# Weight buffers at five different byte offsets, and linear attention begun six parts of a step later

## The chip, the cores and the metric

The kernel runs on one core of a Trainium2 chip. The metric is the device time of one execution in microseconds (us). Before the change it is 2220.42 us, the median of 3 runs (2219.68 to 2222.28).

## What is computed

A two-layer decoder trunk on 256 tokens with 2048 channels, in float32. The reference, cut to its skeleton:

```
for layer in range(2):
    h = rmsnorm(x, norm_mix_g[layer])
    if layer == 0: mix = conv_gla_mixer(h, ...)      # short convolution and gated linear attention
    else:          mix = dilated_attention(h, ...)   # 16 heads, three dilated windows
    x = x + mix
    x = x + square(relu(rmsnorm(x, norm_mlp_g[layer]) @ w1[layer])) @ w2[layer]
return rmsnorm(x, final_norm_g)

def conv_gla_mixer(h, ...):
    a_b, a_c, a_x, q, k, v, r, g_low = split(h @ w_in)
    y_conv = a_b * causal_short_conv(a_c * a_x, conv_w)
    log_a  = log_sigmoid(g_low @ w_gate2 + b_gate) / 16
    o = rmsnorm(gla_chunked(q, k, v, log_a), gla_norm_g) * silu(r)
    return concat([y_conv, o]) @ w_out
```

Nearly all of the work is the products with the large weight matrices: `w_in`, `w_out`, `w_qkv`, `w_o`, and `w1` and `w2` of both MLPs (D_FF is 8192).

## The kernel before

**Weights in steps.** The weights stream through in 769 steps, all but one (step 8, the small gate weight) of one 128x1024 float32 block (512 KB). `load` brings a block into one of four `raw` buffers through the SP queue. `split_high` (ScalarE, L139) writes the block rounded to float32r into a buffer `wh`; `split_low` (VectorE, L152) writes what the rounding left off into a buffer `wl`. There are five buffers of each (WB = 5), used in turn. The loop at L796 splits four steps ahead (LA = 4).

**The products.** A step of the commonest kind ("a", `sub_a`) makes 24 matmuls of 256 columns: for each of 8 pieces of the block the three products `wh` x high, `wh` x low and `wl` x high of an activation tile (`xs`, `ys` or `hs`, whose high and low halves lie side by side). All go through `mm`, so all stand under L155. The weights are the loaded (stationary) operand, the activations the streamed one. Steps of kind "b" (the v projections) have the roles the other way round, with 512 columns streamed.

**Parts.** The loop cuts a step into four parts (j = 0 to 3; six matmuls each in kind "a"). After each part `advance()` counts one and resumes at most one background generator whose time has come. `spawn(gen, after)` enters a generator that starts `after` parts later, and a generator's `yield n` puts it off by n parts. So the place of all small work in the engines' queues (norm factors, gates, linear attention, attention heads) is fixed by counting parts when the program is written, not at run time.

**Linear attention.** `evac_glow` leads, through `after_norm` and `gates`, to the log gates `la`: small matmuls `pz`, then Abs, Exp and Ln on ScalarE (L428 to L430), then two operations on VectorE (L433). `gla_pair(pair)` handles two heads; its first work is four plain float32 matmuls `pg` that read `la` (L446), then `G` (L450), and from there eight rounds of exponentials (`E`), products (`W`) and scores (`psc`), and at the end `po`, `pos` and `porb`. Pair 0 is entered by the trigger at the first step after its v projection (step 17), six parts later; pair 1 in the same way at step 49. Such plain float32 matmuls also occur at the norm factors (`pss`, `prb`) and in the attention heads.

**Addresses.** Tiles of a pool lie one behind the other in the order in which their tags are first asked for. `fill` (88 floats) brings the `const` pool, with `x`, `xs`, `ys` and `hs`, to a multiple of 2 KiB, and `fill2` (16 floats) puts everything in the weight pool 64 bytes past one: all four `raw`, all five `wh` and all five `wl` buffers lie at 64 modulo 2048. The activation halves `xs`, `ys` and `hs` lie at 0 and 1024.

Of the kernel before, what the change touches and what calls it, by code (L numbers as in the profile page):

```python
# [11 lines left out]
F32 = mybir.dt.float32  # L12
F32R = mybir.dt.float32r
# [5 lines left out]
P = 128  # L19
# [30 lines left out]
def trunk_kernel(ctx: ExitStack, tc, xin, vecs, w_in, w_gate, w_gate2, w_out, w_qkv, w_o, w1, w2, w2f,  # L50
# [9 lines left out]
    wts = ctx.enter_context(tc.tile_pool(name="wts", bufs=1))  # L60
# [4 lines left out]
    RAW, WB, LA, WARM = 4, 5, 4, 5  # L65
# [7 lines left out]
    ident, cums = cm[:, 0, :], cm[:, 1, :]  # L73
    ones = small.tile([P, 1], F32, name="ones")
    small.tile([P, 88], F32, name="fill")
    wts.tile([P, 16], F32, name="fill2")
    x = const.tile([P, NK, T], F32, name="x")

# [30 lines left out]
    steps = []  # L109

    def add(g):
        for i in range(g.n):
            steps.append((g, i))

    raws, his, los = {}, {}, {}

    def parts(s):
        return (slice(0, 512), slice(512, 1024)) if s == 0 else (slice(0, 1024),)
# [11 lines left out]
    def split_high(s):  # L130
        if steps[s][0].kind == "h":
            r = raws[s][:, :256].rearrange("p (k c) -> p k c", c=16)
            for q in range(4):
                act.activation(wg3[q][:, :, :16], r[:, 4 * q:4 * q + 4, :], AF.Copy)
            his[s] = None
            return
        his[s] = wts.tile([P, 1024], F32R, tag="wh", bufs=WB, name=f"wh{s}")
        for c in parts(s):
            act.activation(his[s][:, c], raws[s][:, c], AF.Copy)  # L139

    def split_low(s):
        r = raws.pop(s)
        if steps[s][0].kind == "h":
            r = r[:, :256].rearrange("p (k c) -> p k c", c=16)
            for q in range(4):
                dve.tensor_tensor(wg3[q][:, :, 32:48], r[:, 4 * q:4 * q + 4, :],
                                  wg3[q][:, :, :16].bitcast(F32), op=OP.subtract)
            los[s] = None
            return
        los[s] = wts.tile([P, 1024], F32R, tag="wl", bufs=WB, name=f"wl{s}")  # L150
        for c in parts(s):
            dve.tensor_tensor(los[s][:, c], r[:, c], his[s][:, c].bitcast(F32), op=OP.subtract)  # L152

# [93 lines left out]
    def spawn(gen, after=1):  # L247
        bg.append([gen, clock[0] + after])
# [125 lines left out]
    def evac_qk(pair):  # L374
        def f(j, p):
            if j == 0:
                gl["q", pair] = gpool.tile([P, 2, T], F32, tag="gq", bufs=2, name="gq")
                gl["k", pair] = gpool.tile([P, 2, T], F32, tag="gk", bufs=2, name="gk")
            u = grab(p) if pair == 0 else p

            def rest():
                if j < 2:
                    dve.scalar_tensor_tensor(gl["q", pair][:, j, :], u, DK ** -0.5, R["b"],
                                             op0=OP.mult, op1=OP.mult)
                else:
                    dve.tensor_tensor(gl["k", pair][:, j - 2, :], u, R["b"], op=OP.mult)
            if pair == 0:
                spawn(after_norm(rest))
            else:
                rest()  # L390
        return f
# [7 lines left out]
    def evac_v(store, i):  # L399
        def f(tt, p):  # L400
            if tt == 0:
                store[i] = (ap_["p"] if ap_ else gpool).tile([P, 2, 512], F32, tag="v", bufs=2, name="v")
            act.activation(store[i][:, tt, :], p, AF.Copy, scale=R["c"][:, tt:tt + 1])
        return f
# [171 lines left out]
    def evac_r(half):  # L576
        def f(j, p):
            u = grab(p)
            n = 4 * half + j

            def rest():
                if n == 0:
                    gl["r"] = gpool.tile([P, 8, T], F32, name="r")
                pool.tensor_tensor(gl["r"][:, n, :], u, R["b"], op=OP.mult)
            later.append(rest)
        return f
# [139 lines left out]
    triggers = {}  # L726

    for pair in range(2):
        add(Group(w_in, 32 * pair, 8, "a", X, evac_qk(pair)))
        if pair == 0:  # L730
            add(Group(w_gate, 0, 1, "h", X, evac_glow))
        add(Group(w_in, 32 * pair + 8, 8, "b", X, evac_v(gl["v"], pair)))
        triggers[len(steps)] = lambda pair=pair: spawn(gla_pair(pair), 6)
        if pair == 0:
            add(Group(w_in, 16, 8, "a", X, evac_r(0)))
            add(Group(w_in, 24, 8, "a", X, evac_r(1)))
# [30 lines left out]
    for s in range(LA):  # L767
        first_scale(s)
        split_high(s)
        split_low(s)  # L770
        load_x(s + 4)
        load(s + RAW)
# [23 lines left out]
    for s, (g, i) in enumerate(steps):  # L796
# [6 lines left out]
        if s + LA < len(steps):  # L803
            split_high(s + LA)
        f, n = SUB[g.kind]
        wh, wl = his.pop(s), los.pop(s)
        for j in range(n):
            f(g, i, j, wh, wl)
            if j == 1:
                if s + LA < len(steps):  # L810
                    split_low(s + LA)
                if s + LA + RAW < len(steps):
                    load(s + LA + RAW)
            flush()
            if i == g.n - 1:
                if g.kind == "a" and j % 2 == 1:
                    g.evac(j - 1, part_of(g, j - 1))
                    g.evac(j, part_of(g, j))
                    del g.ps[j // 2]
                elif g.kind == "b" and j % 2 == 1:  # L820
                    g.evac(j // 2, g.ps.pop(j // 2))
                elif g.kind == "g" and j == n - 1:
                    g.evac(0, g.ps.pop(0)[:, :T])
                elif g.kind == "h" and j == n - 1:
                    g.evac(0, g.ps.pop(0))
            advance()
# [100 lines left out]
```

## Time and profile before

| | |
|---|---|
| median of 3 runs | 2220.42 us (2219.68 to 2222.28) |
| the profiled execution | 2219.53 us, of it 2217.7 us span |
| TensorE matmuls (PE) busy | 2199.1 us, 99%, 18358 instructions |
| weight loads (PEld) busy | 2167.6 us, 98% |
| VectorE (DVE) busy | 1323.4 us, 60% |
| ScalarE (ACT) busy | 1038.6 us, 47% |
| mean transfer rate | 185 GB/s |

A busy share of PE says only that some matmul was under way, not how fast matmuls followed each other. A window of the trace gives that: the length of the window over the number of matmuls in it. A plain float32 matmul stands in the trace as two, so `pg` with its four is "x8".

### The profile page before, as it was taken

The page shows a single profiled execution, that of the slowest core. Times are in us where ns is not written, and L with a number is a line of the kernel's source. Part 1 is how long each engine was busy: PE and PEld are TensorE (multiplying, and loading weights), DVE is VectorE, ACT ScalarE, POOL GpSimd, SP SyncE. Part 2 cuts the span into 40 slices and gives each one's busy share as a digit, 9 for nine tenths or more (in the row PEclk, how much of TensorE's full clock was granted, in tenths as well). Part 3 has the DMA queues.
Part 4 walks back from the last instruction along what each step waited for, and adds up shares of the span by engine and source line. Part 5 has one row for each costly group of instructions (what it writes and reads, how often), then busy time and mean ns, then how long its engine had stood idle before and what let it go on. Part 6 is the DMA issues. An engine that isn't in the chain of part 4 may idle for free.

```text
span 2217.7 us, 43336 instructions
## 1 busy us (share of the span) xinstructions
PE 2199.1 (99%) x18358; PEld 2167.6 (98%) x18358; DVE 1323.4 (60%) x1813; ACT 1038.6 (47%) x1416; POOL 69.5 (3%) x75
## 2 busy tenths in 40 slices
PE   9999999999999999999999999999999999999997
PEld 8899999999999999999999999999999999999997
DVE  7566666565555555555755565665555555555555
ACT  5555545453444444354544444545434434534443
POOL 4000230000000000000000000000000000000000
PEclk9999999999999999999999999999999999999999
DMA  7455565666566566656565555565655665566653
GB/s 255 144 170 170 163 199 185 197 192 205 191 198 192 190 198 191 198 179 207 184 194 173 170 165 181 168 198 182 190 184 187 190 183 189 173 200 180 192 189 114
DMA packets 114293, 410.97 MB, mean 185 GB/s; under 512 B 12817, under 2 KB 13329, under 8 KB 114098
## 3 DMA queue, kind: packets, MB, share of 16 engines
q1 hardware_dynamic: 113616, 407.55, 57.9%
q8 instruction: 143, 2.34, 0.4%
q10 hardware_dynamic: 482, 0.65, 0.1%
q14 instruction: 52, 0.43, 0.1%
HBM read 406.05 MB, written 2.10 MB: 184 GB/s over the span
## 4 chain that ended last, share of the span: by engine, by line
PE 98%; DVE 1%; issue 0%; DMA 0%; ACT 0%; SPq 0%; DVEq 0%; ACTq 0%
PE acc L155 88%; PE accv L155 6%; PE accg L155 1%; PE psc L507 1%; PE pao L155 0%; DVE xs L258 0%; PE pqk L642 0%; DVE wl L152 0%; DMA raw<-w_in 0%; PE po L155 0%; PE ppt L669 0%; DVE xf L835 0%; PE pqk L641 0%; PE pos L155 0%; PE pg L446 0%
## 5 line engine op out<-in xcount | busy, mean ns | idle before, releaser
L152 DVE TENSOR_TENSOR wl<-raw,wh 128x1024 fp32r<-128x1024 f32 (+1 forms) x769 | 936.0, 1229 | 733.9 <-ACT wh L139 731.7
L139 ACT ACTIVATE wh<-raw 128x1024 fp32r<-128x1024 f32 (+1 forms) x769 | 810.2, 1058 | 880.5 <-PE acc L155 782.7
L155 PE MATMUL acc<-xs,wh 128*128 128x256 f32 x6400 | 1109.9, 279 | 1.4 <-ACT wh L139 1.1
L155 PEld LDWEIGHTS acc<-xs,wh 128*128 128x128 f32 x6400 | 970.9, 189 | 3.7 <-ACT wh L139 1.9
L155 PE MATMUL acc<-xs,wl 128*128 128x256 f32 x3200 | 882.6, 278 | 1.3 <-DVE wl L152 1.3
L155 PE MATMUL acc<-hs,wh 128*128 128x256 f32 x3968 | 687.7, 278 | 0.0
L155 PEld LDWEIGHTS acc<-hs,wh 128*128 128x128 f32 x3968 | 604.6, 189 | 0.0
L155 PEld LDWEIGHTS acc<-xs,wl 128*128 128x128 f32 x3200 | 597.4, 188 | 1.8 <-DVE wl L152 1.5
L155 PE MATMUL acc<-hs,wl 128*128 128x256 f32 x1984 | 552.4, 278 | 0.0
L155 PEld LDWEIGHTS acc<-hs,wl 128*128 128x128 f32 x1984 | 372.4, 188 | 0.0
L155 PE MATMUL acc<-ys,wh 128*128 128x256 f32 x1024 | 177.6, 278 | 0.0
L155 PEld LDWEIGHTS acc<-ys,wh 128*128 128x128 f32 x1024 | 155.3, 189 | 0.1
L155 PE MATMUL acc<-ys,wl 128*128 128x256 f32 x512 | 142.4, 278 | 0.0
L155 PE MATMUL accv<-wh,xs 128*128 128x512 f32 x384 | 121.0, 396 | 0.0
L330 DVE TENSOR_TENSOR hs<-u,hs 128x256 fp32r<-128x256 f32 x128 | 54.5, 425 | 79.0 <-ACT hs L329 79.0
L155 PEld LDWEIGHTS acc<-ys,wl 128*128 128x128 f32 x512 | 96.1, 188 | 0.0
L329 ACT ACTIVATE hs<-u 128x256 fp32r<-128x256 f32 x128 | 53.4, 417 | 70.1 <-DVE u L697 70.1
L155 PEld LDWEIGHTS accv<-wh,xs 128*128 128x128 f32 x384 | 70.7, 188 | 15.0 <-issue 0.8
L155 PE MATMUL accv<-wl,xs 128*128 128x512 f32 x192 | 75.5, 393 | 0.0
L343 DVE TENSOR_TENSOR x<-x,t 128x256 f32<-128x256 f32 x128 | 54.4, 425 | 4.4
L697 DVE TENSOR_TENSOR u<-u 128x256 f32<-128x256 f32 x128 | 53.5, 418 | 0.0
L341 DVE TENSOR_TENSOR t<-acc,rb 128x256 f32<-128x256 f32 x124 | 51.7, 417 | 0.0
(152 smaller groups left out, 782.4 us busy)
## 6 DMA issues: line engine op xcount, KB each, us to landing
raw<-w SPq DMA_DIRECT2D x504, 512.0 KB, 4.2
raw<-w_qkv SPq DMA_DIRECT2D x96, 512.0 KB, 3.6
raw<-w_in SPq DMA_DIRECT2D x95, 512.0 KB, 3.8
raw<-w_out SPq DMA_DIRECT2D x32, 512.0 KB, 4.1
raw<-w_o SPq DMA_DIRECT2D x32, 512.0 KB, 3.8
raw<-w2f SPq DMA_DIRECT2D x8, 512.0 KB, 3.6
x<-xin SPq DMA_DIRECT2D x8, 256.0 KB, 5.2
out_dram<-xf SPq DMA_DIRECT2D x7, 256.0 KB, 2.3
```

The costliest lines, as they stand in the source:

```text
L139: act.activation(his[s][:, c], raws[s][:, c], AF.Copy)
L152: dve.tensor_tensor(los[s][:, c], r[:, c], his[s][:, c].bitcast(F32), op=OP.subtract)
L155: pe.matmul(out_, lhsT=lhsT, rhs=rhs, start=start, stop=stop, skip_group_check=True)
L329: act.activation(t[:, :T], v, AF.Copy)
L330: dve.tensor_tensor(t[:, T:], v, t[:, :T].bitcast(F32), op=OP.subtract)
L341: dve.tensor_tensor(t, p, R["b2"], op=OP.mult)
L343: dve.tensor_tensor(x[:, k, :], x[:, k, :], p, op=OP.add)
L507: pe.matmul(p[:, (2 * h + tt) * P:(2 * h + tt + 1) * P], lhsT=l[:, h, c], rhs=r[:, h, c], start=True, stop=True)
L697: dve.tensor_tensor(u, u, u, op=OP.mult)
```

## The change

Two edits. First, the buffers `wh` and `wl` get five tags each with one buffer a tag (`wh0` to `wh4`, `wl0` to `wl4`; step s takes number s modulo 5), and ahead of the first use of numbers 1 to 4 a tile of 16 floats (64 bytes) is set aside. So `wh0` and `wl0` stay at 64 modulo 2048, and the next ones lie at 128, 192, 256 and 320. All pools allocated behind the weights (`tmp`, and those of linear attention, attention and the final norm) lie 256 bytes higher. Still a `wh` buffer is reused five steps later, except around step 8, which uses no such buffer. `raw`, `xs`, `ys` and `hs` stay where they were.

Second, both pairs of linear attention are spawned 12 parts after their trigger, where they were spawned 6 after it.

```
@@ split_high
-        his[s] = wts.tile([P, 1024], F32R, tag="wh", bufs=WB, name=f"wh{s}")
+        if 0 < s < WB:
+            wts.tile([P, 16], F32, name=f"stagger{s}")
+        his[s] = wts.tile([P, 1024], F32R, tag=f"wh{s % WB}", bufs=1, name=f"wh{s}")
@@ split_low
-        los[s] = wts.tile([P, 1024], F32R, tag="wl", bufs=WB, name=f"wl{s}")
+        los[s] = wts.tile([P, 1024], F32R, tag=f"wl{s % WB}", bufs=1, name=f"wl{s}")
@@ the triggers
-        triggers[len(steps)] = lambda pair=pair: spawn(gla_pair(pair), 6)
+        triggers[len(steps)] = lambda pair=pair: spawn(gla_pair(pair), 12)
```

On TensorE, before, in step 18 (the digits after `wh` and `wl` are the step's), `pg` of pair 0 stands between the step's second and third part:

```order
L155 MATMUL acc0_722<-xs2_137,wh18_654 128x256 x2
L155 MATMUL acc0_722<-xs2_137,wl18_662 128x256
L155 MATMUL acc0_722<-xs3_143,wh18_654 128x256 x2
L155 MATMUL acc0_722<-xs3_143,wl18_662 128x256
L446 MATMUL pg_772<-cm_73,la_695 128x128 x4
L155 MATMUL acc1_723<-xs2_137,wh18_654 128x256 x2
L155 MATMUL acc1_723<-xs2_137,wl18_662 128x256
```

After the change, on TensorE, it stands between steps 19 and 20 (all line numbers from the `wh` lines on are three higher there):

```order
L158 MATMUL acc1_727<-xs4_157,wh19_676 128x256 x2
L158 MATMUL acc1_727<-xs4_157,wl19_684 128x256
L158 MATMUL acc1_727<-xs5_163,wh19_676 128x256 x2
L158 MATMUL acc1_727<-xs5_163,wl19_684 128x256
L449 MATMUL pg_818<-cm_73,la_699 128x128 x4
L158 MATMUL acc0_726<-xs6_177,wh20_694 128x256 x2
L158 MATMUL acc0_726<-xs6_177,wl20_707 128x256
```

So 36 matmuls of 256 columns (12 of the other half of step 18, 24 of step 19) now stand ahead of `pg` that stood behind it, and every later matmul of linear attention has moved by as many. The matmuls of the weights themselves stand in the order of before.

On ScalarE the same place reads, before, from the log gates on:

```order
L430 ACTIVATE la_695<-la_695 128x1024
L139 ACTIVATE wh21_720<-raw21_646 128x1024
L139 ACTIVATE wh22_754<-raw22_664 128x1024
L450 ACTIVATE G_789<-pg_772 128x512
L139 ACTIVATE wh23_791<-raw23_682 128x1024
```

and after:

```order
L433 ACTIVATE la_699<-la_699 128x1024
L142 ACTIVATE wh21_724<-raw21_650 128x1024
L142 ACTIVATE wh22_758<-raw22_668 128x1024
L142 ACTIVATE wh23_788<-raw23_686 128x1024
L142 ACTIVATE wh24_823<-raw24_709 128x1024
L453 ACTIVATE G_841<-pg_818 128x512
```

Two more weight splits stand ahead of `G`. What leads up to `la` has not moved on any engine, and from the end of pair 1 on (step 81) the order on all engines is the old one. On POOL and in the SP queue nothing has moved at all.

## Rows read from the trace of the kernel before

**Rows 1.** The page: busy time by engine; the ended-last chain's shares by engine.

```profile
PE 2199.1 (99%) x18358; PEld 2167.6 (98%) x18358; DVE 1323.4 (60%) x1813; ACT 1038.6 (47%) x1416; POOL 69.5 (3%) x75
...
PE 98%; DVE 1%; issue 0%; DMA 0%; ACT 0%; SPq 0%; DVEq 0%; ACTq 0%
```

**Rows 2.** Windows around `pg`: us, busy (count) of PE, PEld, DVE, ACT, POOL; PEclk, DMA.

```profile
66.00:69.40 3.40, 0.19 (x3) 0.04 (x1) 0.84 (x2) 3.37 (x5) 0.00 (x0) 0.93 0.00 0
69.40:72.40 3.00, 3.00 (x14) 2.97 (x15) 2.71 (x3) 1.61 (x3) 0.00 (x0) 0.51 0.24 22
72.40:80.00 7.60, 7.60 (x69) 7.60 (x69) 2.61 (x6) 4.18 (x5) 0.00 (x0) 1.00 0.62 198
```

**Rows 3.** Timeline, TensorE, around `pg` of pair 0: start, length, what, [idle before].

```profile
65.91 0.28 PE L155 MATMUL acc<-xs,wl 128*128 128x256 f32 x1
69.39 2.15 PE L446 MATMUL pg<-cm,la 128*128 128x128 f32 x8 [3.21 <-DVE la L433]
71.20 0.77 PE L155 MATMUL acc<-xs,wh 128*128 128x256 f32 x2
71.77 0.41 PE L155 MATMUL acc<-xs,wl 128*128 128x256 f32 x1
71.98 0.56 PE L155 MATMUL acc<-xs,wh 128*128 128x256 f32 x2
```

**Rows 4.** Timeline, `pg` of pair 1, which waits for nothing.

```profile
172.47 1.05 PE L446 MATMUL pg<-cm,la 128*128 128x128 f32 x8
173.27 0.48 PE L155 MATMUL acc<-xs,wh 128*128 128x256 f32 x2
```

**Rows 5.** Timeline, ScalarE and VectorE, the same place as rows 3.

```profile
68.43 1.99 ACT L139 ACTIVATE wh<-raw 128x1024 fp32r<-128x1024 f32 x2
...
68.56 1.29 DVE L433 SCALAR_TENSOR_TENSOR la<-pz,la 128x512 f32<-128x512 f32 x2 [9.24 <-ACT la L430]
69.76 2.35 DVE L152 TENSOR_TENSOR wl<-raw,wh 128x1024 fp32r<-128x1024 f32 x2
```

**Rows 6.** Timeline, the first weighted score of pair 0 and the product it reads.

```profile
81.26 0.41 DVE L494 TENSOR_TENSOR W<-E,gq 128x256 f32<-128x256 f32 x1
...
83.61 1.05 PE L507 MATMUL psc<-W 128*128 128x128 f32 x8
```

**Rows 7.** Windows (columns of rows 2): layer 0 MLP, w_o of layer 1, layer 1 MLP.

```profile
418.00:1098.00 680.00, 680.00 (x6002) 680.00 (x6002) 402.50 (x523) 313.48 (x402) 0.00 (x0) 1.00 0.61 195
...
1411.00:1485.00 74.00, 74.00 (x630) 74.00 (x630) 47.60 (x73) 38.80 (x58) 0.00 (x0) 1.00 0.57 185
...
1498.00:2180.00 682.00, 682.00 (x5793) 1.00 0.59 187
```

**Rows 8.** Groups by line, 430 to 1090, then 1500 to 2180: count | busy, mean ns | idle.

```profile
L155 PE MATMUL acc<-hs,wh 128*128 128x256 f32 x2001 | 340.4, 276 | 0.0
L155 PEld LDWEIGHTS acc<-hs,wh 128*128 128x128 f32 x2002 | 301.4, 188 | 0.0
...
L155 PE MATMUL acc<-hs,wh 128*128 128x256 f32 x1910 | 337.6, 281 | 0.0
L155 PEld LDWEIGHTS acc<-hs,wh 128*128 128x128 f32 x1911 | 295.0, 190 | 0.0
```

**Rows 9.** Timeline, TensorE, norm factors of both MLPs: the small matmuls, the stream after.

```profile
410.48 0.39 PE L155 MATMUL acc<-xs,wh 128*128 128x256 f32 x2
...
410.82 0.50 PE L155 MATMUL pss<-ones,ssq 128*128 128x1 f32 x4
...
411.97 0.40 PE L155 MATMUL acc<-xs,wh 128*128 128x256 f32 x2
...
1490.69 0.50 PE L155 MATMUL pss<-ones,ssq 128*128 128x1 f32 x4
...
1491.48 0.39 PE L155 MATMUL acc<-xs,wh 128*128 128x256 f32 x2
...
1496.58 0.60 PE L310 MATMUL prb<-cm,rc 128*128 128x128 f32 x4
...
1497.38 0.40 PE L155 MATMUL acc<-xs,wh 128*128 128x256 f32 x2
```

## The prediction, made before the changed kernel was run

> **What bounds the kernel now.** I read the page first, then windows of the trace, then the timeline at single places. On the page TensorE is busy 99% of the span and makes up 98% of the chain that ended last [rows 1]; ScalarE and VectorE, at 47% and 60%, wait for it. So there are only two ways to a shorter time: take away one of the few places where TensorE stands still or runs at half clock, or make its matmuls follow each other faster. The change reaches for one of each, and the two have to be judged apart.
>
> The one long standstill away from start and end is at `pg` of linear attention's pair 0. The last weight matmul ahead of it starts at 65.91, `pg` at 69.39, and the row puts 3.21 us of idle time down to the log gates on VectorE [rows 3]. [...] Pair 1 has no such wait: its `pg` starts at 172.47 with no idle time ahead of it [rows 4].
>
> For the pace of the matmuls I divide a window by its count. The MLP of layer 0 makes 6002 matmuls in 680 us, one each 113.3 ns. The MLP of layer 1, the same lines with the same shapes, makes 5793 in 682 us, one each 117.7 ns, and the last projection of layer 1 630 in 74 us, 117.5 ns [rows 7]. So there are two paces, 4.4 ns apart, at a granted clock of 1.00 in both. The groups show them too: a matmul's mean goes from 276 to 281 ns, the loads of `wh` from 188 to 190 ns [rows 8]. And the timeline shows where the pace turns: at plain float32 matmuls. Before `pss` of layer 0 two matmuls take 0.39 us, behind it 0.40; at `pss` of layer 1 it turns the other way (0.39 behind it), and at the following `prb` back to 0.40, where it stays for the rest of the kernel [rows 9]. Between such places it never turns, though the five buffers, the eight pieces of a block and the high and low halves go round all the time.
>
> **Linear attention six parts later.** In front of `pg` now come 36 more matmuls of 256 columns. At 113.3 ns these are 4.08 us, so TensorE reaches `pg` at 65.91 + 0.11 + 4.08 = 70.10 us. The log gates do not depend on anything that moved, and VectorE ends them at 68.56 + 1.29 = 69.85 [rows 5]. The wait is gone, with 0.25 us to spare; were the gates 0.5 us later, it would come back as 0.25 us, not as 3.2.
>
> What that is worth: from 65.91 to 72.38, when the clock is back, TensorE now gets 6 weight matmuls and `pg` done. At the full pace the six are 6 x 0.113 = 0.68 us; `pg` takes 173.27 - 172.47 = 0.80 us at pair 1 [rows 4]; about 0.1 us goes with the first matmul behind it. That is 1.58 us in place of 6.47 [rows 3]: **4.9 us less**, 3.3 of it the wait and the rest the half clock.
>
> What is late next? Two weight splits now stand ahead of `G` on ScalarE, and the splits that were held up behind the log gates (steps 21 and 22) are no longer helped by TensorE standing still. `wh` of these two is there at 68.43 + 1.99 = 70.42 and `wl` at 69.76 + 2.35 = 72.11 [rows 5]; TensorE begins step 21 at 70.10 + 0.9 + 2.72 = 73.7 and step 22 2.7 us later. So they stay covered by 1.6 us or more. The weighted score of pair 0 has its product at 81.26 + 0.41 = 81.67 and starts at 83.61 [rows 6], 1.9 us to spare; the wait in parts between `pg` and it is unchanged, and `G` comes some 1.6 us after `pg` where it now comes 0.4 us after, so even then it is not late. ScalarE's table loads and all of POOL's and SP's work keep their order, so I cost them at nothing. Pair 1 is moved by as much and gains nothing. Bounds of this edit: no gain at all if a wait of 3 us turns up elsewhere, 5.0 us if everything fits.
>
> **Buffers at five offsets.** No instruction is added, none moved, the same buffers are waited for. All that can change is how two streams of addresses, the loaded weights and the streamed activations, meet in memory. The trace of before has float32r weight matmuls at one offset only, so no row gives the price. Bounds from the nearest rows: if every long run took the pace of the layer 0 MLP, 5793 x 4.4 ns = 25.5 us and 630 x 4.2 ns = 2.6 us would go, 28 us in the two windows [rows 7], 30 with their edges; the shorter stretches at the slow pace in attention may add 3. If every long run took the slow pace, the layer 0 MLP would lose 6002 x 4.4 = 26.4 us. So the ends are 33 us of gain and some 26 us of loss (46 if all the projections in the slower pace are added).
>
> Which value? The pace does not turn for whole MLPs while pieces at 64, 576, 1088 and 1600 and halves at 0 and 1024 meet in every combination, and a change of pace needs a float32 matmul in between. Those rows speak for a state of the engine rather than for addresses; the order of the float32 matmuls from step 81 on is unchanged, and so the runs behind them should keep the pace they have. I take **0** as the single likeliest value. But bits of the address below 512 bytes have never varied in this trace, and just those are changed now, so this is the weak step.
>
> [...]
>
> **The sum.** On the profiled execution 2219.5 - 4.9 = 2214.6 us; the median lies 0.9 above that execution, so **2215.5 us** for the median of after.
>
> **The rivals.**
> One, the offsets end the slow pace. For it: the slow pace is a lock that lasts 680 us undisturbed, and a new address relation every 24 matmuls would be the first thing in it to disturb it. The weight loads, of all things, are the rows that lengthen (188 to 190 ns) while it lasts [rows 8]. In full it gives 2215.5 - 30 = 2185, down to 2182 with the attention stretches. In part, if only some of the steps change pace, 2190 to 2212.
> Two, on the other side: the offsets take the layer 0 MLP out of its fast pace. For it: the fast run exists only at offset 64, and four fifths of the buffers leave that offset. In full it gives 2215.5 + 26.4 = 2242. It decides against the change once the steps at the slow pace outnumber those of before by 4.9 us / (24 x 4.4 ns) = 46 of the 768; if two of the five offsets prove slow in the runs that are fast now, it comes to about 2226.
> Three, the first edit doesn't bring what it should, because the log gates or `G` are late again: 2219 to 2221.
>
> **How the numbers follow.** Forecast (2213.5 to 2217) 0.35; rival one in full 0.27, in part 0.16; rival two 0.17; rival three 0.05. The range 2181 to 2232 leaves out the upper half of rival two and little else. About 0.2%, or 4.4 us, is what a measurement of this kernel can tell from no change, so the line is at 2216.0, right beside the forecast. Faster: 0.43 of rival one and 0.21 of the forecast's 0.35, 0.64. Same: 0.14 and 0.04, 0.18. Slower: 0.18.
>
> **What would show it.** The first edit: no idle time ahead of `pg`, a granted clock of 1.00 in the window behind it, and the second layer's work 4.9 us earlier. The second: the counts of matmuls in windows of both MLPs. If they stand at 113.3 and 117.7 ns as before, the forecast holds; if both stand at 113.3, rival one; if pace varies from step to step with the number of the buffer, addresses matter and the forecast's weak step was wrong. A pace below 113.3 ns anywhere would show that I had misread the fast pace as the floor.

## The result, and the profile after

The changed kernel takes **2242.19 us**, the median of 3 runs (2242.11 to 2242.67), against 2220.42 before: a ratio of 1.0097 with a 95% interval of 1.0074 to 1.012. It is slower by 1%, and outside the predicted range of 2181 to 2232.

The page of after, busy time by engine and the shares of the chain that ended last, as in [rows 1]:

```profile
PE 2225.3 (99%) x18358; PEld 2192.9 (98%) x18358; DVE 1324.9 (59%) x1813; ACT 1040.6 (46%) x1416; POOL 64.2 (3%) x75
...
PE 98%; DVE 1%; DMA 0%; issue 0%; SPq 0%; ACT 0%; DVEq 0%; ACTq 0%
```

The same 18358 matmuls, PE busy for the same 99%, and 26.2 us more of it (2225.3 for 2199.1). The other engines have nearly their old busy times. So nothing new is waited for; the matmuls themselves follow each other more slowly.

**Around `pg`** the delay (the second edit in "The change"; the prediction calls it the first) did what was forecast. Windows of after (us, busy (count) of PE, PEld, DVE, ACT and POOL, then PEclk and DMA), which answer to [rows 2]:

```profile
66.00:70.00 4.00, 4.00 (x36) 4.00 (x35) 0.51 (x1) 3.96 (x5) 0.00 (x0) 1.00 0.00 0
70.00:72.50 2.50, 2.50 (x24) 2.50 (x24) 2.50 (x4) 2.50 (x4) 0.00 (x0) 1.00 0.00 0
```

and the timeline of after, TensorE and VectorE, which answers to [rows 3, 5] (start, length, what, and in brackets the idle time before it):

```profile
68.19 0.41 PE L158 MATMUL acc<-xs,wh 128*128 128x256 f32 x2
...
68.56 0.39 PE L158 MATMUL acc<-xs,wh 128*128 128x256 f32 x2
...
71.17 0.28 PE L158 MATMUL acc<-xs,wl 128*128 128x256 f32 x1
71.29 1.05 PE L449 MATMUL pg<-cm,la 128*128 128x128 f32 x8
72.09 0.48 PE L158 MATMUL acc<-xs,wh 128*128 128x256 f32 x2
...
69.49 1.29 DVE L436 SCALAR_TENSOR_TENSOR la<-pz,la 128x512 f32<-128x512 f32 x2 [9.26 <-ACT la L433]
```

PE is busy throughout, `pg` has no idle time ahead of it, and the granted clock is 1.00 where it was 0.51 in the window behind the standstill [rows 2]. The log gates end at 69.49 + 1.29 = 70.78, 0.51 us ahead of `pg`. The first two lines show something else: at 68.56 the pace turns from slow to fast between two weight steps, with no float32 matmul anywhere near. [rows 9] never show that.

**The pace.** Windows in both MLPs, well inside the stretches of [rows 7] (here and below: us, PE busy (count), PEclk, DMA share, GB/s):

```profile
440.00:1080.00 640.00, 640.00 (x5487) 1.00 0.60 190
1535.00:2160.00 625.00, 625.00 (x5359) 1.00 0.60 188
```

That is 640 us / 5487 = 116.6 ns and 625 us / 5359 = 116.6 ns, at a granted clock of 1.00, where before stood 113.3 and 117.7. The two paces of before are gone, and one between them stands in both layers. It is a mean of different steps. Windows of five consecutive steps of layer 0, cut at the first matmul of each, buffers at 64, 128, 192, 256 and 320 in this order (a step has 24 matmuls; the counts take in those that reach over an edge):

```profile
604.74:607.46 2.72, 2.72 (x26) 1.00 0.53 193
607.46:610.30 2.84, 2.84 (x27) 1.00 0.63 185
610.30:613.13 2.83, 2.83 (x27) 1.00 0.03 6
613.13:616.01 2.88, 2.88 (x26) 1.00 0.34 81
616.01:618.74 2.73, 2.73 (x27) 1.00 1.02 375
```

So the pace goes with the number of the buffer. From the starts of all matmuls of some 49 steps at each offset in layer 0, one matmul takes 113.5 ns at 64, 118.2 at 128, 117.9 at 192, 120.3 at 256 and 113.5 at 320, and each is within 0.3 ns in layer 1.

**Where the 21.8 us come from.** Between the starts of the same steps in both traces:

| stretch (steps) | before | after | difference |
|---|---|---|---|
| linear attention and the projections beside it (17 to 132) | 346.9 | 350.4 | +3.6 |
| layer 0 MLP (132 to 385) | 689.3 | 709.5 | +20.2 |
| projections and attention of layer 1 (385 to 518) | 396.5 | 400.7 | +4.3 |
| layer 1 MLP (518 to 768) | 707.0 | 700.6 | -6.4 |

Together +21.6 us of the 23.1 between the two profiled executions (2242.67 and 2219.53); the rest lies ahead of step 17 and behind step 768.

### The profile page after: what moved, and what is told of

It is laid out like the page before. It is cut to its first block, busy times and chain, and to the rows that moved or that the text cites. A ratio compares the mean times of both kernels' runs of the same rounds, so it can differ in the third digit from the quotient of the medians.

```text
span 2240.9 us, 43333 instructions
## 1 busy us (share of the span) xinstructions
PE 2225.3 (99%) x18358; PEld 2192.9 (98%) x18358; DVE 1324.9 (59%) x1813; ACT 1040.6 (46%) x1416; POOL 64.2 (3%) x75
## 4 chain that ended last, share of the span: by engine, by line
PE 98%; DVE 1%; DMA 0%; issue 0%; SPq 0%; ACT 0%; DVEq 0%; ACTq 0%
PE acc L158 88%; PE accv L158 6%; PE accg L158 1%; PE psc L510 1%; PE pao L158 0%; DVE xs L261 0%; DMA raw<-w_in 0%; PE pqk L645 0%; DVE wl L155 0%; PE po L158 0%; PE ppt L672 0%; DVE xf L838 0%; PE pqk L644 0%; PE pos L158 0%; PE prb L313 0%
## 5 line engine op out<-in xcount | busy, mean ns | idle before, releaser
L158 PE MATMUL acc<-xs,wh 128*128 128x256 f32 x6400 | 1126.0, 280 | 1.6 <-ACT wh L142 1.3
```

What stands on the lines that cost most here:

```text
L158: pe.matmul(out_, lhsT=lhsT, rhs=rhs, start=start, stop=stop, skip_group_check=True)
```

## Experiments

Where nothing else is said, each kernel is after with only the edit shown, and so has linear attention 12 parts late. The kernel before ran beside them on the same chips, with medians of 2220.4 to 2221.3 us. A time without a range is that of one execution.

**The two edits apart.** First the delay alone: before with 12 in place of 6 in the two spawns.

> The kernel before with linear attention begun 12 parts after its trigger, all weight buffers at 64 modulo 2048. Theory one (the byte offset sets the pace of the weight matmuls, and the delay is worth its 4.9 us): 2215.5 us, the MLP of layer 0 at 113.3 ns a matmul, that of layer 1 at 117.8. Rival (the delay shifts where the small float32 matmuls fall and so turns the long runs to another pace): layer 0 at 117.8 ns and about 2242 us.

Measured: 2215.37 us (2215.0 to 2215.78), ratio 0.9975 (0.9965 to 0.9984). Steps 17 to 132 take 341.8 us in place of 346.9, and from step 132 on every stretch of the table above is as before to 0.01 us. The timeline has `pg` without idle time, and the gates ending at 69.04 + 1.29 = 70.33, 0.25 us ahead of it:

```profile
70.58 1.05 PE L446 MATMUL pg<-cm,la 128*128 128x128 f32 x8
...
69.04 1.29 DVE L433 SCALAR_TENSOR_TENSOR la<-pz,la 128x512 f32<-128x512 f32 x2 [9.25 <-ACT la L430]
```

So this edit is worth 5.0 us, and what is left, 2242.19 - 2215.37 = **26.8 us, is the price of the offsets**. From the other side, after with 6 in the spawns:

> The five offsets 64 to 320 with linear attention begun 6 parts after its trigger. Theory one (the offsets bring the loss): the paces by buffer of the changed kernel, 113.5 ns at 64 and 320 and 118 to 120 ns at 128, 192 and 256, and about 2242.2 + 4.9 = 2247 us. Rival (the delay brings the loss): about 2220 us.

Measured: 2248.73 us (2247.42 to 2248.83), ratio 1.0125 (1.0108 to 1.0142), with the pace of after in both MLPs (5488 and 5359 in the windows). By the medians the delay is worth 6.5 us there, so the two edits add up within 2 us. In the profiled execution, the fastest of the four, steps 17 to 132 take 355.5 us against 350.4 in after, 5.1 us.

**Is it the change of offset, or the offset?** A buffer at 64 and one at 320 are equally quick in after. This kernel gives every buffer a multiple of 256 bytes past 64 (64, 320, 576, 832, 1088):

```
+    PADH = (0, 64, 64, 64, 64)      # floats ahead of wh0 to wh4
...
-        if 0 < s < WB:
-            wts.tile([P, 16], F32, name=f"stagger{s}")
+        if s < WB and PADH[s]:
+            wts.tile([P, PADH[s]], F32, name=f"stagger{s}")
```

> The delay kept, and the five offsets 64, 320, 576, 832 and 1088, which differ by 256 bytes. Theory one (an offset has its own pace, and what counts is the offset modulo 256): 113.4 ns in the MLP of layer 0; in layer 1 either 113.4 ns too (if a step to another offset ends the slow pace; about 2186 us) or 117.8 (if it doesn't; about 2215 us). Rival (a change of offset between one step and the next is what costs): 116 to 118 ns in both MLPs, about 2240 us.

Measured: 2215.37 us (2215.09 to 2215.85), ratio 0.9978 (0.9969 to 0.9988), the same as the delay alone. The windows are those of the delay alone too, to the matmul:

```profile
440.00:1080.00 640.00, 640.00 (x5649) 1.00 0.61 193
1535.00:2160.00 625.00, 625.00 (x5309) 1.00 0.58 186
```

113.3 and 117.7 ns. So going from buffer to buffer by 256 bytes neither costs anything nor ends the slow pace; of these offsets only the remainder by 256 counts. The other half of the question is one offset for all, 192, with nothing changing from step to step: `PADH = (32, 0, 0, 0, 0)`.

> The delay kept, and all ten weight buffers at 192 modulo 2048, so that no offset changes from step to step. Theory one (an offset has its own pace): 117.9 ns in both MLPs, as at 192 in the changed kernel, and about 2215.5 + 27 + 4 = 2247 us. Rival (the change of offset costs): 113.3 ns in layer 0 as at 64 throughout, about 2215 us.

Measured: 2258.64 us. Both MLPs run at 117.7 ns (windows: 5436 in 640 us and 5309 in 625 us). It is slower than expected by 12 us because the work outside the MLPs, which the expectation put at 4 us, is slow here as well: against the delay alone steps 17 to 132 lose 10.7 us and the projections and attention of layer 1 5.9. An unchanging offset makes the layer 0 MLP slow. The same at 256, `PADH = (48, 0, 0, 0, 0)`:

> The delay kept, all ten weight buffers at 256 modulo 2048. Theory one (an offset has its own pace): about 120 ns in both MLPs, as at 256 in the changed kernel, and some 2215.4 + 6.7 x 6002 + 2.2 x 5976 ns and 10 for the projections = about 2280 us. Rival (the change of offset from step to step costs): 113.3 ns in layer 0, 2215 us.

Measured: 2293.35 us, the slowest of all:

```profile
440.00:1080.00 640.00, 640.00 (x5336) 1.00 0.58 185
1535.00:2160.00 625.00, 625.00 (x5211) 1.00 0.58 183
```

119.9 ns in both layers, a third pace. The groups of the window 440 to 1080 (count | busy us, mean ns of one | idle) against [rows 8] show a matmul at 283 and a load at 192 ns, where before has 276 and 188 in its layer 0 MLP:

```profile
L159 PE MATMUL acc<-hs,wh 128*128 128x256 f32 x1664 | 299.7, 283 | 0.0
L159 PEld LDWEIGHTS acc<-hs,wh 128*128 128x128 f32 x1665 | 259.8, 192 | 0.0
```

So it is the offset itself, and no step from one to the next.

**Finer steps.** Buffers at 32, 96, 160, 224 and 256 modulo 512, `PADH = (120, 16, 16, 16, 8)`:

> The delay kept, and the five offsets 32, 96, 160, 224 and 256 modulo 512. Theory one (each offset has its own pace, the same modulo 256): 120 ns at 256 again, and four paces between 113.3 and 121 ns that the trace gives at a cost of one run; an offset that holds 113.3 ns or less in both MLPs would be the better one. Rival (an offset has no pace of its own, the order of the offsets has): 256 at another pace than 120.3 ns, since it now stands behind 224 and not behind 192.

Measured: 2271.84 us (5401 and 5275 in the windows, 118.5 ns). By buffer, from the starts of the matmuls: 118.3 at 32, 118.8 at 96, 119.6 at 160, 116.6 at 224, 119.5 at 256. None reaches 113.3. At 256 stand 119.5 here and 120.3 in after, beside other neighbours, so the neighbouring steps seem to leave a small trace; no run isolates it.

**Weights alone, or weights against activations?** Raising `fill` from 88 to 104 floats puts the activations 64 bytes higher and the weights with them, at 128; `PADH` is 0 throughout.

> The delay kept; the activations and all weight buffers lie 64 bytes higher, so the activations at 64 and 1088 and the weights at 128 modulo 2048, 64 bytes apart as before. Theory one (what counts is how the addresses of the loaded weights and of the streamed activations lie to each other): the paces of the kernel with the delay alone, 113.3 ns in layer 0 and 117.8 in layer 1, about 2215 us. Rival (the weights' own offset counts): 118 ns or more in both, as at 128 in the changed kernel, 2245 us or more.

Measured: 2189.38 us. The layer 0 MLP keeps 113.3 ns with its weights at 128, the offset that costs 118.2 in after:

```profile
440.00:1080.00 640.00, 640.00 (x5649) 1.00 0.60 193
1535.00:2160.00 625.00, 625.00 (x5517) 1.00 0.59 193
```

The stretches ahead of and behind it are those of the delay alone too (341.8 us for steps 17 to 132, 396.6 in place of 396.5 for the projections and attention of layer 1). So it is not the weights' own offset that counts, but how they lie to what moved with them.

Two things moved with them: the streamed activations, and the `raw` buffers from which ScalarE and VectorE make the weights, and which lie at 64 in every other kernel. The trace of the kernel with all weights at 256 speaks against `raw`, and against the other engines and DMA altogether. A window of it in which neither VectorE, ScalarE, GpSimd nor a DMA works (columns as in [rows 2]), and the matmuls in it:

```profile
613.14:613.60 0.46, 0.46 (x6) 0.46 (x5) 0.00 (x0) 0.00 (x0) 0.00 (x0) 1.00 0.00 0
...
613.16 0.40 PE L159 MATMUL acc<-xs,wh 128*128 128x256 f32 x2
613.40 0.28 PE L159 MATMUL acc<-xs,wl 128*128 128x256 f32 x1
613.52 0.40 PE L159 MATMUL acc<-xs,wh 128*128 128x256 f32 x2
```

Three matmuls still take 613.52 - 613.16 = 0.36 us, 120 ns each. In steps 140 to 385 of that trace, 679 matmuls begin while ScalarE and VectorE are both idle and 763 while both work, and both sorts take 120.0 ns from start to start. What is left is how weights and activations lie to each other, shown for this one shift of both.

Layer 1 turned fast as well, which was not expected; the timeline shows how. Behind `pss` the slow pace stays, and the `prb` that follows turns it to fast; in [rows 9] `pss` turned it to fast and `prb` back to slow.

```profile
1486.13 0.40 PE L159 MATMUL acc<-xs,wh 128*128 128x256 f32 x2
1486.49 0.50 PE L159 MATMUL pss<-ones,ssq 128*128 128x1 f32 x4
...
1487.29 0.40 PE L159 MATMUL acc<-xs,wh 128*128 128x256 f32 x2
...
1492.59 0.61 PE L314 MATMUL prb<-cm,rc 128*128 128x128 f32 x4
...
1493.39 0.39 PE L159 MATMUL acc<-xs,wh 128*128 128x256 f32 x2
```

**Do the float32 matmuls turn the pace?** All offsets at 64, and at the end of attention, ahead of layer 1's MLP, two plain float32 matmuls of one column into a bank that nothing reads:

```
+        if pair == 7:
+            p = bank("turn")
+            for tt in range(2):
+                mm(p[:, tt:tt + 1], ident, ones, True, True)
```

> The delay kept, all weight buffers at 64, and two plain float32 matmuls of one column (which change nothing that is read) set behind the last attention heads, in the last projection of layer 1. Theory one (at an offset of 64 there are two paces, and float32 matmuls of this kind turn one into the other): the projection runs at 113.3 ns from there on, the norm's two turns leave the MLP of layer 1 at 113.3 in place of 117.8 ns, and the time is 2215.4 - 26.7 - 3 + 0.5 = about 2186 us. Rival (the pace of layer 1 has another cause): 2215 to 2216 us.

Measured: 2186.83 us (2186.38 to 2187.36), ratio 0.9845 (0.9828 to 0.9861). The timeline at the added matmuls:

```profile
1404.11 0.40 PE L159 MATMUL acc<-ys,wh 128*128 128x256 f32 x2
...
1404.46 0.50 PE L159 MATMUL turn<-ones,cm 128*128 128x1 f32 x4
...
1405.26 0.39 PE L159 MATMUL acc<-ys,wh 128*128 128x256 f32 x2
```

The pace is slow ahead of them and fast behind, and with one more turn in the row the layer 1 MLP comes to lie in the fast pace (5517 in 625 us, 113.3 ns). The two matmuls give back 28.5 us against the delay alone. So the state that [rows 9] suggested is real too.

**High and low parts at different offsets.** `wh` at 64 and `wl` at 192 modulo 512, everything else as in the delay alone (`PADL` is set aside ahead of each `wl` as `PADH` is ahead of each `wh`):

```
+    PADH = (0, 96, 96, 96, 96)      # ahead of each wh
+    PADL = (32, 32, 32, 32, 32)     # ahead of each wl
```

> The delay kept, all wh buffers at 64 and all wl buffers at 192 modulo 512. Theory one (each weight load has its pace by its own address): between the two, some 115 ns in layer 0, since one load in three is of wl; about 2226 us. Rival (the two kinds must lie alike, the wl loads drag the others along): 117.8 ns in both MLPs, about 2245 to 2258 us.

Measured: 2184.15 us, which neither theory had forecast. The same kernel, timed in four executions beside the kernel before:

> The kernel with wl at 192 and wh at 64 modulo 512 and the delay, timed in rounds. Theory one (with the two kinds of weights 128 bytes apart the lasting slow pace does not occur): 2184 us, both MLPs at 113.3 ns, after every float32 matmul a short slow stretch only. Rival (the fast pace of layer 1 was luck of one execution): some executions at 2184 and some near 2211 us.

2183.86 us (2183.52 to 2184.1), ratio **0.9832** (0.9816 to 0.9849): faster than both kernels. Windows of the two MLPs:

```profile
440.00:1080.00 640.00, 640.00 (x5650) 1.00 0.61 193
1535.00:2160.00 625.00, 625.00 (x5517) 1.00 0.60 191
```

and the timeline at layer 1's `pss`:

```profile
1481.61 0.50 PE L162 MATMUL pss<-ones,ssq 128*128 128x1 f32 x4
...
1482.77 0.40 PE L162 MATMUL acc<-xs,wh 128*128 128x256 f32 x2
...
1483.12 0.39 PE L162 MATMUL acc<-xs,wh 128*128 128x256 f32 x2
```

That is 113.3 ns in both layers. Behind `pss` the slow pace still comes, but by 1483.12, 1.5 us after `pss` began, it has fallen back to the fast one by itself. Two more pairs, to see whether any pair that differs does this: `wh` at 64 with `wl` at 128, and the mirror, `wh` at 192 with `wl` at 64.

> The delay kept, wh at 64 and wl at 128 modulo 512. Theory one (a pace belongs to the pair of offsets, not to each load): no forecast of the pair, but one pace throughout each MLP, between 113.3 and 120 ns. Rival (each load brings the pace of its own offset): one load in three at the 118.2 ns of 128, so 115 ns in layer 0 and 115 to 118 in layer 1.

Measured: 2266.57 us, 118.2 ns in both layers (5416 and 5290 in the windows).

> The delay kept, the two kinds changed over: wh at 192, wl at 64 modulo 512. Theory one (a pace belongs to the pair, 128 bytes apart): 113.3 ns in both MLPs, about 2184 us. Rival (wh, with two loads in three, sets the pace, and 192 is a slow offset): 117.8 ns in both, about 2258 us.

Measured: 2272.19 us, 118.8 ns (5385 and 5260). `wh` stands in two matmuls of three. If each part kept the pace of its own offset in after, the first kernel would come to (2 x 113.5 + 118.2) / 3 = 115.1 ns and the second to (2 x 117.9 + 113.5) / 3 = 116.4. Both are above that, the second above either of its parts. So the pace is not a mean of prices by address; it belongs to the two parts together. Nor is the pair symmetrical.

All settings side by side (weights' bytes modulo 256, activations at 0 except in the second row; pace in the MLPs of layers 0 and 1):

| `wh` | `wl` | ns per matmul | time, us |
|---|---|---|---|
| 64 (or 64 to 1088 by 256) | the same | 113.3 and 117.7 | 2215.4 |
| 128, activations at 64 | 128 | 113.3 and 113.3 | 2189.4 |
| 64, two float32 matmuls added | 64 | 113.3 and 113.3 | 2186.8 |
| 64 | 192 | 113.3 and 113.3 | 2183.9 |
| five offsets of after | the same | 116.6 and 116.6 | 2242.2 |
| 192 | 192 | 117.7 and 117.7 | 2258.6 |
| 64 | 128 | 118.2 and 118.2 | 2266.6 |
| five offsets by 32 | the same | 118.5 and 118.5 | 2271.8 |
| 192 | 64 | 118.8 and 118.8 | 2272.2 |
| 0 | 0 | 119.9 and 119.9 | 2293.4 |

## Why the prediction was wrong

**What bounds the kernel** was right: TensorE's pace and the one standstill, nothing else. Every difference above is one of the two.

**Linear attention six parts later** was right: -4.9 us forecast, -5.0 measured with the delay alone; 0.25 us to spare at `pg` forecast, 0.25 measured; splits, `G` and the weighted scores covered, as no idle time shows up elsewhere. Rival three, that it brings nothing, fell.

**Buffers at five offsets** was wrong, and the step that failed is "Which value?". It read [rows 7] and [rows 9] as speaking "for a state of the engine rather than for addresses" and took 0. The runs showed +26.8 us. Both halves of that reading can be named now. That there is a state, turned by plain float32 matmuls, is right: two added ones moved a whole MLP from 117.7 to 113.3 ns. That addresses therefore don't matter did not follow. The pieces at 64, 576, 1088 and 1600 and the halves at 0 and 1024 meet in all combinations, but they are all alike in their remainder by 256, and the runs show that just this counts (in after 113.5 ns at 64 and at 320, but 118.2 at 128, 117.9 at 192 and 120.3 at 256). Those rows varied what makes no difference and could say nothing on what does. The prediction noted that address bits below 512 had never varied, and still took the middle of its bounds for the likeliest value; the observation should have taken the weight off 0 and put it on the two ends.

Nor do transfers set the pace by buffer: their share in the five steps shown goes from 0.03 to 1.02 and the pace follows the buffer, not the share (the steps at 64 and 320 take 2.72 and 2.73 us at shares of 0.53 and 1.02).

**Rival two** (0.17) is what happened in sign and, at 2242, to the microsecond in size, but the size is a coincidence of its terms. It put 26.4 us on the layer 0 MLP and nothing elsewhere. That MLP lost 20.2, because two of the five offsets, 64 and 320, stay at 113.5 and because the other three are not all at 117.8 but at up to 120.3. The layer 1 MLP gained 6.4 us in place of 0, since those two offsets are fast there as well. And against the delay alone the stretches of steps 17 to 132 lost 8.6 us and those of layer 1's attention another 4.3. The "two of five offsets slow" that gave 2226 was three of five, and slower than the slow pace of before.

**Rival one** (the offsets end the slow pace) fell in its full form. A change of address every step does not disturb it: 64 and 320 in turn left 117.7 in layer 1. In part it is true by the 6.4 us.

**The range** ended at 2232 because the upper half of rival two was left out. Its bounds were too narrow as well: both ends were made of the two paces seen, and 119.9 ns, which no row of before has, gives 2293 us when all buffers share that offset.

**What would show it** named the sign that came: "if pace varies from step to step with the number of the buffer, addresses matter". A pace below 113.3 ns was not seen at any offset.

## What to carry to other kernels

Where TensorE is busy for 99% of the span, divide the length of a window by its matmuls, stretch by stretch: two paces of the same instructions are a gain in waiting (here 2220 to 2184 us, by padding that puts high and low weights 128 bytes apart, and six parts of delay), and a busy share shows none of it (99% here at 2220 and at 2242 us). A row excludes a cause only if the cause varied in it; before calling addresses irrelevant, ask by which power of two the addresses seen differ. And try one uniform offset before several different ones, since a mixture of good and bad offsets shows a mean that looks like either (116.6 ns here, from offsets at 113.5 to 120.3).

## What the runs showed of the hardware

In these runs, at a granted clock of 1.00, the pace of the float32r matmuls of 256 columns, each with its own weight load, depended on where the loaded weights lie against the streamed activations: a buffer at 128 took 118.2 ns in after, with the activations at 0 and 1024, and all weights at 128 took 113.3 in both MLPs with them at 64 and 1088 (the one shift of both that was run). Offsets 256 bytes apart acted alike (64, 320, 576, 832 and 1088, with 113.3 and 117.7 ns as at 64 alone; tried from 64 alone). The best pace was 113.3 ns; all weights at 256, with the activations at 0 and 1024, took 119.9.

With all weights 64 bytes past the activations there were two lasting paces, 113.3 and 117.7 ns, and plain float32 matmuls could turn one into the other; two of one column were enough, ahead of the layer 1 MLP (117.7 to 113.3). With the high part at 64 and the low part at 192 only the fast one lasted, 113.3 ns in both MLPs.

What in the memory or in TensorE makes 256 bytes the period, why the two parts act as a pair, and why only one way round, stays open: the rows show starts and lengths of matmuls, nothing of the reads inside them. Whether a group of float32 matmuls always turns the pace isn't settled either; the `pss` ahead of the layer 1 MLP in the kernel with everything 64 bytes higher did not (two matmuls took 0.40 us ahead of it and behind it). Its loaded operand `ssq` lies 64 bytes higher there too, and only `ones` where it lay, so the offsets of the float32 operands may count as well; no run tried that.
